# The residual's pieces of x in the FFN's gate and convolution tiles, squares of h over them, two buffers for the other squares

## The chip, the cores and the metric

The kernel runs on one core of one Trainium2 chip. The metric is the device time of one execution in microseconds (us). Of the kernel before there are three timed runs and one profiled execution.

## The reference

One inference step of one layer on 2048 frames of a prompt and 32 frames of a running stream, 1024 features wide. A mixer (stick-breaking attention with 8 heads of 64, and a state-space group) and a gated feed-forward network (FFN, width 2816, with a causal convolution of width 3 on the gate branch), each between two RMS norms. What this case touches is the sandwich of norms:

```python
def rmsnorm(x, g):
    x32 = x.astype(jnp.float32)
    y = x32 * lax.rsqrt(jnp.mean(x32 * x32, axis=-1, keepdims=True) + NORM_EPS)
    return (y * g.astype(jnp.float32)).astype(x.dtype)

# h = x + RMSNorm_post(Mixer(RMSNorm_pre(x)))
# y = h + RMSNorm_post2(ConvFFN(RMSNorm_pre2(h)))
```

The kernel must give y, the new keys and values, and the new states of the scan and of both convolutions, in float32.

## The kernel before

**Layout and precision.** Features lie on the 128 partitions, frames on the free axis. x, h and y are eight pieces of 128 features (c = 0 to 7). A dense matmul has float32 accuracy from three passes: both operands are split into a high and a low part (`xhi`, `xlo`, `w`), in `Kernel.dense` (L118 to L133; the matmuls are L124). Weights are split once, written back to HBM (`wS_out`, `wS_up`, `wS_dn`) and read from there later. The sums stand in PSUM tiles `o` and `u`, and in the last part of the program `t`.

**Stages.** The frames are cut into four super-blocks s = 0 to 3 of 512, 512, 512 and 544 columns. After the input projections, `Attention.heads` runs for each super-block in turn. Into the attention of super-block s+1 is woven, step by step, the rest of the work of super-block s: `Tail.stream`, a generator, which `Attention.fill` advances at a rate of its steps over the attention's slots. The stream of the last super-block runs alone at the end (`Tail.alone`).

**Attention in one line.** For each slot: scores z on PE (L811, two PSUM tiles), two sigmoids on ACT (`gam` L659, `beta` L660), a scan on DVE (`prow` L662), a product on POOL or DVE (L667), a transposition on PE (`pt` L832) and its copy (`wt` L835), then the sum over values (`pa` L847). A z tile is free again only when the scan that reads its first column is done.

**One stream.** A super-block has a half a and a half b of 256 columns (272 in the last). `Tail.stream` gives, in this order: eight steps of what the previous super-block still owes of its down projection; the output projection of half a (`out_units`, into tiles `m`, with squares of m summed in `msq`); the output projection of half b, with a step of the residual of half a after every fourth of its steps; the norm of h of half a (`root`); the residual of half b in one go; `split` of both halves into `xhi` and `xlo` (L958, L959); the norm of half b; the rest of what is owed; then `up` and `down` of the FFN by groups of columns, with steps of `finish` of the super-block before between them. What is left of the last down projection is owed to the next stream, and in the last super-block it is done at once, tile by tile, each with its `finish`.

**Residual** (L928 to L947). The norm's factor goes into `rm` (L201 in `rstd_steps` writes it). Then for each of the eight pieces: a tile `xr` (two buffers in the attention's scratch pool, eight in the pool `tl_late` for the last super-block; L938), the load of x from HBM (L939, in SP's queue), the scale of m by the gain and by `rm` (L940, DVE), the addition of x (L944, POOL for even c, DVE for odd c), the store of h to scratch in HBM (`hS`, L945, SP's queue), and the square of h.

**Square** (L764 to L772). The first square of a sum is written by ACT straight into it (L768). Every other is written by ACT into `sqt`, one buffer (L770, L771), and added by POOL (L772). Callers are the attention's output (`sq`), the output projection and the residual (`msq`), and `square_f` for the FFN's output (`fsq`).

**Up, down, finish.** `up` computes the gate column in `gb` (two buffers, 548 wide), its convolution in `y` (two buffers, 546 wide), the GeLU in steps on ACT, DVE and POOL (L1003 to L1013), and leaves `ah` and `al`. Between the last `up` of one super-block and the first of the next, `gb` and `y` hold nothing. `down` adds its sums to the tiles f, one buffer each: the first group is copied (L1057, ACT), the others are added (L1059, DVE). `finish` (L1067 to L1086) is the norm and residual of the FFN's output: factor `rstdf`, load of h into an `xr` tile (L1079), scale (L1080, DVE), addition (L1084), store of y. A new super-block's first copy into f waits for the stores of y of the one before.

**Order.** Each engine works through its instructions in one order, which a scheduler of the tile framework fixes when the program is built, from its own model of times and from the tiles that are free; a DMA is issued by SP in SP's order. Matmuls of the stream are held behind the last score or transposition written before them (`pin`).

Of the kernel before, what the change touches and what calls it, by code (L numbers as in the profile page):

```python
# [8 lines left out]
F32 = mybir.dt.float32  # L9
# [3 lines left out]
ALU = mybir.AluOpType  # L13
# [10 lines left out]
P = 128  # L24
# [584 lines left out]
class Attention:  # L609
# [151 lines left out]
                nc.gpsimd.tensor_tensor(lo[c][:, c0:c1], x, hi[c][:, c0:c1].bitcast(F32), op=ALU.subtract)  # L761
        return hi, lo

    def square(self, sq, x, first):  # L764

        nc = self.kn.nc
        if first:
            nc.scalar.activation(sq, x, AF.Square)  # L768
        else:
            t = self.tmp.tile([P, 272], F32, name="sqt")[:, : sq.shape[-1]]  # L770
            nc.scalar.activation(t, x, AF.Square)  # L771
            nc.gpsimd.tensor_tensor(sq, sq, t, op=ALU.add)  # L772

# [105 lines left out]
class Tail:  # L879
# [48 lines left out]
    def residual(self, s, half):  # L928

        kn, nc, att = self.kn, self.kn.nc, self.att  # L930
        t0 = SBS[s][0]
        c0, c1 = half
        n = c1 - c0
        rm = att.tmp.tile([P, 272], F32, name="rstd")
        kn.rstd_narrow(att.tmp, *kn.bank, [self.msq[:, c0:c1]], n, D, out=rm)
        yield
        for c, m in enumerate(self.m):
            x = (self.late or att.tmp).tile([P, 272], F32, name="xr", bufs=8 if self.late else 2)  # L938
            nc.sync.dma_start(x[:, :n], kn.a["xT"][:, c, t0 + c0 : t0 + c1])  # L939
            nc.vector.scalar_tensor_tensor(  # L940
                m[:, c0:c1], m[:, c0:c1], kn.col(C_GMIXP + c), rm[:, :n], op0=ALU.mult, op1=ALU.mult
            )
            eng = nc.vector if c % 2 else nc.gpsimd
            eng.tensor_tensor(m[:, c0:c1], m[:, c0:c1], x[:, :n], op=ALU.add)  # L944
            nc.sync.dma_start(kn.hS[s][:, c, c0:c1], m[:, c0:c1])  # L945
            att.square(self.msq[:, c0:c1], m[:, c0:c1], c == 0)
            yield  # L947

    def split(self, s, half):
# [118 lines left out]
    def finish(self, s, c0, c1, f):  # L1068

        kn, nc, att = self.kn, self.kn.nc, self.att  # L1070
        t0, n = SBS[s][0], c1 - c0
        r = att.tmp.tile([P, 272], F32, name="rstdf")
        for _ in kn.rstd_steps(
            att.tmp, *kn.bank, [self.fsq[:, c0:c1]], n, D, out=r, of=self.cols.pop((s, c0))
        ):
            yield
        for c in range(KC):
            h = (self.late or att.tmp).tile([P, 272], F32, name="xr", bufs=8 if self.late else 2)
            nc.sync.dma_start(h[:, :n], kn.hS[s][:, c, c0:c1])  # L1079
            nc.vector.scalar_tensor_tensor(  # L1080
                f[c][:, c0:c1], f[c][:, c0:c1], kn.col(C_GFFNP + c), r[:, :n], op0=ALU.mult, op1=ALU.mult
            )
            eng = nc.vector if c % 2 else nc.gpsimd
            eng.tensor_tensor(f[c][:, c0:c1], f[c][:, c0:c1], h[:, :n], op=ALU.add)  # L1084
            nc.sync.dma_start(kn.o["yT"][:, c, t0 + c0 : t0 + c1], f[c][:, c0:c1])
            yield  # L1086
# [208 lines left out]
```

## Time and profile before

| | us |
|---|---|
| median of three runs | 2998.81 |
| lowest and highest | 2997.21, 3003.68 |
| the profiled execution, its own time | 2999.56 |
| span in it, first to last instruction | 2997.4 |
| output projection of super-block 0, first residual's scales | from 812.27 |
| the last f squares of super-block 2, in the part that runs alone | 2560.9 to 2590.4 |

The mean granted clock of TensorE over the span is 0.979 of full speed. Engines: PE = TensorE matmul, PEld = its weight loads, DVE = VectorE, ACT = ScalarE, POOL = GpSimd, SP = SyncE, whose queue issues the DMAs (SPq). A row of the timeline reads: start, length, engine, line, operation, output <- inputs, shape, count, and in brackets the idle time just before it and what ended that. In a table of windows each engine has its busy time and its count of instructions, then come the granted clock, the share of DMA and GB/s.

### The profile page before, as it was taken

What the parts mean: (1) busy time and instruction counts of PE and PEld (TensorE: products, weight loads), DVE (VectorE), ACT (ScalarE), POOL (GpSimd) and SP (SyncE); (2) the same over time, 40 slices, a digit from 0 to 9 for tenths busy, and PEclk for the clock granted to TensorE, in tenths of its full rate; (3) what the DMA queues carried; (4) which work ended last, traced back from release to release, by engine and by line L of the source; (5) the groups of instructions that cost most, each with busy time, mean ns of one, the idle gap of its engine ahead of it and who ended that gap; (6) DMA issues with size and microseconds to landing.
All of it is one profiled execution on the core that took longest, in us unless ns stands there. A gap on an engine that the chain in (4) does not pass through costs nothing.

```text
span 2997.4 us, 43276 instructions
## 1 busy us (share of the span) xinstructions
PE 2839.3 (95%) x16175; PEld 2320.3 (77%) x16175; DVE 1567.7 (52%) x2386; ACT 1239.6 (41%) x2514; POOL 1254.8 (42%) x1077
## 2 busy tenths in 40 slices
PE   8999899989979999999999999999999999899996
PEld 6777778866757778886677777856777779799996
DVE  7676676546574544337734344485444543523334
ACT  5344444346675544337533333564333433312111
POOL 4555555245666665536522222454122224511113
PEclk9999999989989999999999999999999999899998
DMA  5645453657657777876455545645544455554555
GB/s 172 183 145 177 144 169 106 185 150 248 241 178 242 246 250 266 289 265 203 158 190 176 184 156 208 232 163 174 177 165 167 157 196 191 192 188 167 178 178 171
DMA packets 234659, 571.58 MB, mean 191 GB/s; under 512 B 49514, under 2 KB 101362, under 8 KB 205906
## 3 DMA queue, kind: packets, MB, share of 16 engines
q1 hardware_dynamic: 234450, 568.81, 57.2%
q8 instruction: 129, 2.11, 0.3%
q14 instruction: 80, 0.66, 0.1%
HBM read 435.22 MB, written 133.50 MB: 190 GB/s over the span
## 4 chain that ended last, share of the span: by engine, by line
PE 72%; DVE 14%; DMA 6%; issue 3%; ACT 3%; POOL 2%; SPq 1%; DVEq 0%; POOLq 0%; ACTq 0%
PE o L124 36%; PE u L124 11%; PE t L124 10%; PE pa L847 4%; PE z L811 3%; PE pt L832 3%; DVE prow L662 2%; PE o L365 2%; DVE xc L341 2%; DVE acB L436 1%; DMA xr<-hS 1%; DMA acB<-acD 1%; DVE xc L337 1%; DVE x L263 1%; DMA w<-wS_out 1%
## 5 line engine op out<-in xcount | busy, mean ns | idle before, releaser
L124 PE MATMUL o<-xhi,w 128*128 128x512 f32 (+2 forms) x3968 | 1039.6, 346 | 28.4 <-ACT xhi L287 7.9
L124 PEld LDWEIGHTS o<-xhi,w 128*128 128x128 f32 x3968 | 696.5, 191 | 129.6 <-issue 10.1
L124 PE MATMUL o<-xlo,w 128*128 128x512 f32 (+2 forms) x1984 | 684.9, 345 | 9.4 <-DVE xlo L959 4.1
L109 POOL TENSOR_TENSOR w<-wraw,w 128x1024 fp32r<-128x1024 f32 (+2 forms) x156 | 370.6, 2376 | 256.1 <-ACT w L108 233.3
L124 PEld LDWEIGHTS o<-xlo,w 128*128 128x128 f32 x1984 | 379.6, 191 | 56.8 <-DVE xlo L959 7.6
L667 POOL TENSOR_TENSOR beta<-beta,prow 128x512 f32<-128x512 f32 (+3 forms) x256 | 255.7, 1000 | 377.4 <-DVE prow L662 345.2
L124 PE MATMUL u<-xhi,w 128*128 128x512 f32 x1056 | 345.8, 398 | 0.8 <-ACT r L201 0.5
L124 PE MATMUL o<-ah,w 128*128 128x512 f32 x992 | 335.9, 401 | 3.3 <-ACT f L1057 2.6
L1013 POOL TENSOR_TENSOR y<-y,gb 128x512 f32<-128x512 f32 (+1 forms) x88 | 115.5, 1313 | 511.2 <-ACT gb L1012 509.2
L662 DVE TENSOR_TENSOR_SCAN prow<-gam,prow,z 128x513 f32<-128x513 f32 x192 | 244.8, 1277 | 108.7 <-ACT beta L660 103.2
L124 PEld LDWEIGHTS u<-xhi,w 128*128 128x128 f32 x1056 | 198.5, 188 | 56.1 <-issue 5.6
L659 ACT ACTIVATE gam<-z 128x512 f32<-128x512 f32 (+2 forms) x320 | 173.3, 542 | 128.1 <-PE z L811 83.0
L124 PEld LDWEIGHTS o<-ah,w 128*128 128x128 f32 x992 | 187.1, 189 | 49.8 <-ACT f L1057 3.6
L124 PE MATMUL u<-xlo,w 128*128 128x512 f32 x528 | 209.3, 396 | 0.0
L835 ACT COPY wt<-pt 128x512 f32<-128x512 f32 (+3 forms) x282 | 148.1, 532 | 144.0 <-PE pt L832 141.3
L1005 DVE SCALAR_TENSOR_TENSOR y<-gb,cv,y 128x512 f32<-128x512 f32 (+1 forms) x176 | 162.3, 923 | 78.4 <-ACT y L1003 75.6
L108 ACT CAST w<-wraw 128x1024 fp32r<-128x1024 f32 (+2 forms) x156 | 155.2, 995 | 114.5 <-PE o L124 63.7
L124 PE MATMUL o<-al,w 128*128 128x512 f32 x496 | 196.5, 396 | 0.0
L124 PE MATMUL t<-xhi,w 128*128 128x272 f32 x960 | 189.1, 292 | 2.3 <-DMA w<-wS_up 2.0
L832 PEld LDWEIGHTS pt<-ident,beta 128*128 128x128 f32 x1088 | 132.4, 144 | 67.8 <-issue 27.5
L832 PE MATMUL pt<-ident,beta 128*128 128x128 f32 x1088 | 177.4, 282 | 6.4 <-POOL beta L667 3.9
L124 PE MATMUL t<-ah,w 128*128 128x272 f32 (+1 forms) x768 | 160.1, 302 | 17.4 <-ACT f L1057 7.5
(262 smaller groups left out, 4845.9 us busy)
## 6 DMA issues: line engine op xcount, KB each, us to landing
w<-wS_up SPq DMA_DIRECT2D x132, 1024.0 KB, 4.8
w<-wS_dn SPq DMA_DIRECT2D x72, 768.0 KB, 4.8
wS_up<-w SPq DMA_DIRECT2D x44, 1024.0 KB, 4.8
w<-wS_out SPq DMA_DIRECT2D x39, 1024.0 KB, 6.3
wraw<-wup SPq DMA_DIRECT2D x44, 512.0 KB, 5.9
k<-kS SPq DMA_DIRECT2D x80, 256.0 KB, 4.0
wS_dn<-w SPq DMA_DIRECT2D x24, 768.0 KB, 4.5
w<-wS_dn SPq DMA_DIRECT2D x32, 512.0 KB, 4.4
```

The costliest lines, as they stand in the source:

```text
L108: nc.scalar.copy(hi[:, :n, :], raw[:, :n, :])
L109: nc.gpsimd.tensor_tensor(lo[:, :n, :], raw[:, :n, :], hi[:, :n, :].bitcast(F32), op=ALU.subtract)
L124: mm = nc.tensor.matmul(ps[:, : c1 - c0], l[:, k, :], at(r, k0 + k)[:, c0:c1], start=first and i == 0 and k == 0, stop=last and i == 2 and ...
L659: nc.scalar.activation(g[:, c0:512], z, AF.Sigmoid, scale=-0.125)
L662: nc.vector.tensor_tensor_scan(back(pr), back(g), z[:, 0:1].to_broadcast([P, n + 1]), self.kn.ones[:, 0:1] if prev is None else prev, op0= ...
L667: eng.tensor_tensor(b[:, :n], b[:, :n], pr[:, c0 + 1 : 513], op=ALU.mult)
L811: mm = nc.tensor.matmul(z[:, :n], q[:, P * b : P * b + P], k[:, :n], start=e == 0, stop=e == 1 and kc < s)
L832: mm = nc.tensor.transpose(t[:, P * j : P * j + P], w[:, P * j : P * j + P], kn.ident[:])
L835: copy(wt[:, : n // P, P * b : P * b + P], t[:, :n].rearrange("p (i q) -> p i q", q=P))
L847: nc.tensor.matmul(av[DH * (j % 2) : DH * (j % 2) + DH, c0:], v[:, j, :], wt[:, j, c0:], start=kc == s and j < 2, stop=kc == 0 and j > 1,)
L1005: nc.vector.scalar_tensor_tensor(y[:, :W], gb[:, i : i + W], kn.col(wc + i), y[:, :W], op0=ALU.mult, op1=ALU.add)
L1013: nc.gpsimd.tensor_tensor(y[:, :W], y[:, :W], t, op=ALU.mult)
```

## The change

`residual` takes, in the first three super-blocks, its pieces of x into the tiles `gb` and `y` of the FFN: pieces 0 and 1 into the two halves of a `y` tile, 2 and 3 into those of a `gb` tile, 4 and 5 into the second `y`, 6 and 7 into the second `gb`. In the last super-block the eight `xr` tiles stay. In all four the square of h is written over the piece of x, which has just been added, and not into `sqt`. `sqt` has two buffers for the other squares, and `finish` uses the name of the residual's factor (`rstd`) for its own. Behind L764 line numbers are higher by one, behind the residual by six.

```diff
--- before.py
+++ after.py
@@ -761,13 +761,14 @@
                 nc.gpsimd.tensor_tensor(lo[c][:, c0:c1], x, hi[c][:, c0:c1].bitcast(F32), op=ALU.subtract)
         return hi, lo
 
-    def square(self, sq, x, first):
+    def square(self, sq, x, first, t=None):
 
         nc = self.kn.nc
         if first:
             nc.scalar.activation(sq, x, AF.Square)
         else:
-            t = self.tmp.tile([P, 272], F32, name="sqt")[:, : sq.shape[-1]]
+            if t is None:
+                t = self.tmp.tile([P, 272], F32, name="sqt", bufs=2)[:, : sq.shape[-1]]
             nc.scalar.activation(t, x, AF.Square)
             nc.gpsimd.tensor_tensor(sq, sq, t, op=ALU.add)
 
@@ -935,15 +936,20 @@
         kn.rstd_narrow(att.tmp, *kn.bank, [self.msq[:, c0:c1]], n, D, out=rm)
         yield
         for c, m in enumerate(self.m):
-            x = (self.late or att.tmp).tile([P, 272], F32, name="xr", bufs=8 if self.late else 2)
-            nc.sync.dma_start(x[:, :n], kn.a["xT"][:, c, t0 + c0 : t0 + c1])
+            if self.late:
+                x = self.late.tile([P, 272], F32, name="xr", bufs=8)[:, :n]
+            else:
+                if c % 2 == 0:
+                    pair = self.yp.tile([P, 548], F32, name="gb") if c % 4 else self.yp.tile([P, 546], F32, name="y")
+                x = pair[:, 272 * (c % 2) : 272 * (c % 2) + n]
+            nc.sync.dma_start(x, kn.a["xT"][:, c, t0 + c0 : t0 + c1])
             nc.vector.scalar_tensor_tensor(
                 m[:, c0:c1], m[:, c0:c1], kn.col(C_GMIXP + c), rm[:, :n], op0=ALU.mult, op1=ALU.mult
             )
             eng = nc.vector if c % 2 else nc.gpsimd
-            eng.tensor_tensor(m[:, c0:c1], m[:, c0:c1], x[:, :n], op=ALU.add)
+            eng.tensor_tensor(m[:, c0:c1], m[:, c0:c1], x, op=ALU.add)
             nc.sync.dma_start(kn.hS[s][:, c, c0:c1], m[:, c0:c1])
-            att.square(self.msq[:, c0:c1], m[:, c0:c1], c == 0)
+            att.square(self.msq[:, c0:c1], m[:, c0:c1], c == 0, x)
             yield
 
     def split(self, s, half):
@@ -1069,7 +1075,7 @@
 
         kn, nc, att = self.kn, self.kn.nc, self.att
         t0, n = SBS[s][0], c1 - c0
-        r = att.tmp.tile([P, 272], F32, name="rstdf")
+        r = att.tmp.tile([P, 272], F32, name="rstd")
         for _ in kn.rstd_steps(
             att.tmp, *kn.bank, [self.fsq[:, c0:c1]], n, D, out=r, of=self.cols.pop((s, c0))
         ):
```

How the instructions stand is changed at three places. First SP's queue, around the loads of x for the first half of super-block 0 (`w<-wS_out` are loads of output weights, `hS<-m` the stores of h, `qa`, `k` and `v` belong to attention). Before:

```order
L104 DMA w<-wS_out_7385 128x2048
L945 DMA hS_101<-m_7284 128x256
L939 DMA xr<-xT 128x256
L945 DMA hS_101<-m_7285 128x256
L939 DMA xr<-xT 128x256
L104 DMA w<-wS_out_7436 128x2048
L945 DMA hS_101<-m_7286 128x256
L945 DMA hS_101<-m_7287 128x256
L939 DMA xr<-xT 128x256 x2
L104 DMA w<-wS_out_7486 128x2048
L828 DMA v<-vS_87 128x256
```

The same eight loads in the changed kernel:

```order
L945 DMA y<-xT 128x256 x2
L112 DMA wS_out_7385<-w 128x2048
L107 DMA wraw<-wout 128x1024
L945 DMA gb<-xT 128x256 x2
L945 DMA y<-xT 128x256 x2
L945 DMA gb<-xT 128x256
L807 DMA k<-kS_78 128x512
L945 DMA gb<-xT 128x256
```

Before, all but the first two loads stand one or two at a time behind stores of h; now all eight stand together, 38 to 45 rows of the queue ahead of the first store of h, and among the stores of split weights.

Second, DVE in the same half: the last of the eight scales, the four additions of x and what stands behind them (`prow` is the attention's scan, `xlo` the split). Before:

```order
L940 SCALAR_TENSOR_TENSOR m_7291<-m_7291,cv,rstd 128x256
L944 TENSOR_TENSOR m_7285<-m_7285,xr 128x256
L944 TENSOR_TENSOR m_7287<-m_7287,xr 128x256
L944 TENSOR_TENSOR m_7289<-m_7289,xr 128x256
L859 TENSOR_TENSOR att<-pa,att 64x512
L662 SCALAR_TENSOR_TENSOR prow<-gam_5853,ones,z 128x513
L662 SCALAR_TENSOR_TENSOR prow<-gam_5854,prow,z 128x513
L667 TENSOR_TENSOR beta<-beta,prow 128x512
L944 TENSOR_TENSOR m_7291<-m_7291,xr 128x256
```

In the changed kernel:

```order
L946 SCALAR_TENSOR_TENSOR m_7291<-m_7291,cv,rstd 128x256
L950 TENSOR_TENSOR m_7285<-m_7285,y 128x256
L950 TENSOR_TENSOR m_7287<-m_7287,gb 128x256
L950 TENSOR_TENSOR m_7289<-m_7289,y 128x256
L950 TENSOR_TENSOR m_7291<-m_7291,gb 128x256
L662 SCALAR_TENSOR_TENSOR prow<-gam_5853,prow,z 128x513
L662 SCALAR_TENSOR_TENSOR prow<-gam_5854,prow,z 128x513
L662 SCALAR_TENSOR_TENSOR prow<-gam_5855,ones,z 128x129
```

The fourth addition stood behind two scans and now stands ahead of them.

Third, POOL in the last super-block, around the residual of its half b, where the squares of super-block 2's FFN output (`fsq`) are added. Before:

```order
L944 TENSOR_TENSOR m_22314<-m_22314,xr 128x272
L944 TENSOR_TENSOR m_22316<-m_22316,xr 128x272
L944 TENSOR_TENSOR m_22318<-m_22318,xr 128x272
L944 TENSOR_TENSOR m_22320<-m_22320,xr 128x272
L772 TENSOR_TENSOR msq<-msq,sqt 128x272 x7
L772 TENSOR_TENSOR fsq<-fsq,sqt 128x256
L184 TENSOR_TENSOR rcol_23016<-rcol_23016,mhalf 128x3
L772 TENSOR_TENSOR fsq<-fsq,sqt 128x256 x6
L1013 TENSOR_TENSOR y<-y,gb 128x546 x2
```

In the changed kernel:

```order
L773 TENSOR_TENSOR fsq<-fsq,sqt 128x256 x7
L950 TENSOR_TENSOR m_22248<-m_22248,xr 128x272
L773 TENSOR_TENSOR fsq<-fsq,sqt 128x256
L950 TENSOR_TENSOR m_22250<-m_22250,xr 128x272
L950 TENSOR_TENSOR m_22252<-m_22252,xr 128x272
L950 TENSOR_TENSOR m_22254<-m_22254,xr 128x272
L773 TENSOR_TENSOR fsq<-fsq,sqt 128x256 x2
L773 TENSOR_TENSOR msq<-msq,xr 128x272 x3
L773 TENSOR_TENSOR fsq<-fsq,sqt 128x256
```

Seven of the 14 additions into `fsq` stand ahead of the residual's additions, and the others among its squares; before, all stood behind them.

## The prediction

> **What bounds the kernel now.** I read the page first: its busy shares, its slices, and its chain.
>
> ```profile
> PE 2839.3 (95%) x16175; PEld 2320.3 (77%) x16175; DVE 1567.7 (52%) x2386; ACT 1239.6 (41%) x2514; POOL 1254.8 (42%) x1077
> PE   8999899989979999999999999999999999899996
> PEclk9999999989989999999999999999999999899998
> PE 72%; DVE 14%; DMA 6%; issue 3%; ACT 3%; POOL 2%; SPq 1%; DVEq 0%; POOLq 0%; ACTq 0%
> ```
>
> PE is busy 2839.3 of 2997.4 us, so 158.1 us are idle, and a little more goes where the granted clock falls. The change alters no matmul. All it can win is idle PE time, and the slices (75 us each) show where that lies: the low ones are the twelfth (7, from 824 us), the 35th (8, from 2548 us) and the last (6, from 2923 us), and in the same three PEclk stands at 8. Then I read the waits, summed over the span (engine, line, what it waited for: us in total, times, longest).
>
> ```profile
> DVE m L944 <- DMA xr<-xT: 24.6, 10, 7.7
> PE z L811 <- DVE prow L662: 23.4, 28, 2.4
> ACT sqt L771 <- POOL msq L772: 24.0, 28, 2.2
> ACT sqt L771 <- POOL fsq L772: 21.1, 23, 4.8
> ```
>
> The first row is the wait that the change aims at, on DVE. The second is how DVE's lateness reaches PE: attention's score matmuls (z) wait for the scan (prow) to free one of two PSUM tiles. The last two are the single `sqt` tile: ACT can write the next square only after POOL has added the last one. ACT and POOL are busy 41% and 42% of the span, so these 45.1 us are mostly not on PE's path.
>
> **The change, part by part.** Every load, scale, add, store and square is still there, with the same shape, so nothing is removed and nothing is added: PE's 2839.3 us stay. What moves is when DVE, ACT, POOL and SP's queue do them.
>
> *A: super-block 0, first half.* The timeline of DVE and of SP's queue, and two windows (PE, PEld, DVE, ACT, POOL busy; granted clock; DMA share; GB/s):
>
> ```profile
> 812.27 3.74 DVE L940 SCALAR_TENSOR_TENSOR m<-m,cv,rstd 128x256 f32<-128x256 f32 x8 [4.13 <-ACT rstd L201]
> 819.68 0.43 DVE L944 TENSOR_TENSOR m<-m,xr 128x256 f32<-128x256 f32 x1 [3.34 <-DMA xr<-xT]
> 826.52 0.78 DVE L944 TENSOR_TENSOR m<-m,xr 128x256 f32<-128x256 f32 x1 [6.42 <-DMA xr<-xT]
> 816.73 0.43 SPq L939 DMA_DIRECT2D xr<-xT  x1
> 820.64 0.96 SPq L939 DMA_DIRECT2D xr<-xT  x2
> 828.21 1.45 SPq L939 DMA_DIRECT2D xr<-xT  x2
> 828.00:860.00 32.00, 23.46 (x120) 14.86 (x121) 23.30 (x27) 22.33 (x51) 21.93 (x22) 0.84 0.67 227
> 872.00:896.00 24.00, 18.67 (x85) 12.62 (x82) 20.72 (x31) 15.37 (x38) 14.52 (x19) 0.86 0.49 143
> ```
>
> The eight scales are done in 3.74 us, but with two `xr` tiles the loads are issued one or two at a time until 828.21, and DVE stands still 3.34 + 6.42 = 9.76 us before two of its four adds. The scans queue behind them on the same engine. In 828:860 PE is then idle 32.00 − 23.46 = 8.54 us and loses 23.46 × (1 − 0.84) = 3.75 us to the clock: 12.3 us. With the change the four tiles of the gate pool hold all eight pieces and are idle there, so the loads can be issued before the scales. DVE gets 9.76 us back, ahead of the stretch in which PE starves. Bounds: 0 and −12.3. DVE also has the second half of the out projection's scans to catch up with, whose work is unchanged, so I take half: **−6**.
>
> *B: super-block 0, second half.* In 872:896 PE loses 5.33 us idle and 18.67 × 0.14 = 2.6 us of clock, but DVE is busy 20.72 of 24 us there with scales, adds and the split, none of which goes. I bound this by 0 and half of it, −4, and take **−1**, near the first, since the busy DVE row is the nearer one.
>
> *C: super-blocks 1 and 2.* The two waits and the stretches behind or around them, with DVE's scales and the one stall of PE that the clock follows:
>
> ```profile
> 1346.72 0.68 DVE L944 TENSOR_TENSOR m<-m,xr 128x256 f32<-128x256 f32 x1 [3.15 <-DMA xr<-xT]
> 1924.40 0.43 DVE L944 TENSOR_TENSOR m<-m,xr 128x256 f32<-128x256 f32 x1 [7.68 <-DMA xr<-xT]
> 1389.35 4.33 DVE L940 SCALAR_TENSOR_TENSOR m<-m,cv,rstd 128x256 f32<-128x256 f32 x8
> 1394.92 0.79 PE L811 MATMUL z<-k,qa 128*128 128x512 f32 x1 [2.11 <-DVE prow L662]
> 1388.00:1404.00 16.00, 12.37 (x50) 7.01 (x48) 15.88 (x23) 10.90 (x25) 7.93 (x9) 0.79 0.44 149
> 1962.00:1998.00 36.00, 31.48 (x162) 19.41 (x162) 32.46 (x42) 26.72 (x62) 21.96 (x26) 1.00 0.62 202
> ```
>
> Here DVE waits 3.15 and 7.68 us for x in the first halves. PE pays in the second halves, where DVE is full: 3.63 us idle plus 12.37 × 0.21 = 2.6 us of clock in 1388:1404, that is 6.2, and 4.52 us in 1962:1998, together 10.7 us. In the new order the first half's chain ends sooner, and units of the last down projection that were used up before now stand beside the second half's residual. They are dense matmuls that PE can do while a scan is late. But DVE's load in those stretches (15.88 of 16 us) stays. Bounds 0 and −10.7; half: **−5**.
>
> *D: super-block 3.* The groups, waits and rows of the place where the new block's down projection first writes the f tiles:
>
> ```profile
> 2540.18 0.86 POOL L184 TENSOR_TENSOR rn_v<-rn_v,mhalf 128x3 f32<-128x3 f32 x1 [6.90 <-DVE rn_v L176]
> L772 POOL TENSOR_TENSOR fsq<-fsq,sqt x14: 723/738/1152, 2560.9 to 2589.7; 128x256 f32<-128x256 f32 x14
> 2608.40 5.22 DVE L1080 SCALAR_TENSOR_TENSOR f<-f,cv,rstdf 128x256 f32<-128x256 f32 x8 [0.31 <-ACT rstdf L201]
> ACT f L1057 <- DMA o_yT<-f: 6.9, 2, 5.6
> PE t L124 <- ACT f L1057: 7.5, 1, 7.5
> 2604.00:2620.00 16.00, 8.04 (x48) 7.65 (x47) 9.98 (x25) 3.91 (x11) 6.99 (x7) 0.68 0.74 231
> ```
>
> The 14 squares of super-block 2's f are added between 2560.9 and 2590.4 us, behind the residual's squares, all through one `sqt`. Its final norm therefore ends late (scales at 2608.40), the stores of y later, and the first copy into an f tile waits for them; PE waits 7.5 us for that copy. The window's loss is 7.96 us idle + 8.04 × 0.32 = 2.6 us of clock = 10.5 us. With two `sqt` tiles most of these squares move ahead of the second residual, into time in which POOL waits (6.90 us in one piece), and the final norm can end some 17 us earlier, twice the stall and more. Bounds 0 and −10.5. What replaces the stall is the supply of activations to the same down projection, so I leave a third: **−7**.
>
> *E: the tail.* In the last tile one scale group takes 5.42 us of DVE, and squares go in steps of ACT, then POOL:
>
> ```profile
> 2980.61 0.43 ACT L771 ACTIVATE sqt<-f 128x272 f32<-128x272 f32 x1 [0.87 <-POOL fsq L772]
> 2981.12 0.76 POOL L772 TENSOR_TENSOR fsq<-fsq,sqt 128x272 f32<-128x272 f32 x1 [0.54 <-ACT sqt L771]
> 2974.00:2982.00 8.00, 1.09 (x7) 0.87 (x7) 5.93 (x12) 1.72 (x4) 5.17 (x7) 0.76 0.65 198
> ```
>
> A step of 0.43 + 0.87 = 1.30 us shrinks to POOL's own 0.76 at best, 0.54 each. Seven to eight such steps would give −4, if all are behind the last matmul; PE's gap in 2974:2982 has its cause in DVE (5.93 of 8 us). I take **−1**, bounds 0 and −4.
>
> Edits at nothing: the shared `rstd` name lets the final norm wait for readers of the residual's factor, which are over long before. The gate's tiles are needed again by the first up unit, after the residual's last square; that unit's result needs the norm of those squares anyway, so the wait hides behind it. The cost if the cover goes is one square, 0.76 us.
>
> Sum: −6 − 1 − 5 − 7 − 1 = **−20**. The profiled execution took 2999.56 us (span 2997.4, 2.16 around it), 0.75 above the median of 2998.81 that runs without it show, so 2979.6, rounded to 2980.
>
> **A rule weighed on the clock.** Two 4 us windows show what an interrupted PE costs afterwards:
>
> ```profile
> 880.00:884.00 4.00, 4.00 (x13) 3.32 (x14) 3.38 (x6) 1.50 (x4) 2.56 (x4) 0.50 0.26 79
> 1396.00:1400.00 4.00, 3.21 (x11) 2.37 (x10) 4.00 (x5) 2.39 (x7) 2.36 (x3) 0.50 0.45 131
> ```
>
> Both run at a granted clock of 0.50 although PE is busy. The Trainium skill ("TensorE: Matmul & The Clock Gate", section "HAM oscillation — how this bites in real kernels") says that PE gaps over about 3.4 us bring the half clock. The wait row before the second window is 2.11 us and the idle time of its 16 us is 3.63, so the trace has the half clock behind a shorter single wait too. By the page only gaps over its limit would count: the sum would keep A and D and lose C's 2.6 us of clock, some 1 us less gain in the middle value.
>
> **Rivals.**
>
> *R1, covered anyway (0.14).* DVE's waits for x vanish but PE is limited by DVE's work in these stretches. For it: DVE at 15.88 of 16 us in 1388:1404, which no load changes. Against it: 9.76 us of pure DVE standstill just ahead of 828:860. Only D and E come, −8: 2992.
>
> *R2, nothing comes of it (0.09).* The loads stand behind other entries in SP's queue that wait (weights, the gate's tiles), and land no sooner. For it: PE waits for weights in this place already, 3.78 us in the row below. Against: the four tiles are idle when the residual starts. D's stall would also stay, if the first norm is not what is late. 2999.
>
> ```profile
> 1296.80 0.58 PE L124 MATMUL o<-xhi,w 128*128 128x256 f32 x1 [3.78 <-DMA w<-wS_out]
> L944 DVE TENSOR_TENSOR m<-m,xr x32: 389/430/1503, 815.9 to 2552.6; 128x256 f32<-128x256 f32 x24, 128x272 f32<-128x272 f32 x8
> L944 POOL TENSOR_TENSOR m<-m,xr x32: 723/908/968, 812.8 to 2549.4; 128x256 f32<-128x256 f32 x24, 128x272 f32<-128x272 f32 x8
> ```
>
> *R3, slower by bunching (0.10).* With x always there, eight scales (4.33 us) and four adds (4 × 0.43) stand on DVE in one block of 6 us with no scan between, where a wait used to let the scheduler put scans. PE has two z tiles, some 2 us of cover. Each such block would then make a gap like that of 1388:1404, 6.2 us with its clock. Four new ones, in both halves of super-blocks 1 and 2, cost 25; A and C do not come, D and E give −8: +17, 3016. It decides when the block outlasts z's two tiles by about 3 us. Against it: eight scales in one block exist already (rows 812.27 and 1389.35), and only the second is followed by a gap at once.
>
> *R4, DVE and POOL adds collide (0.05).* Packed adds run on both engines at the same time. DVE's add has a median of 0.430 us and a longest of 1.503, so something holds it at times. If 16 of the 24 adds of the first three super-blocks each lose a POOL add, 0.908, DVE loses 14.5 us in full stretches; A and C are eaten, D, E and B give −9: +5.5, 3005. The Trainium skill ("SBUF — State Buffer", section "Who interferes with whom") says that a DVE instruction with two SBUF inputs and a GpSimd one that reads SBUF hold an exclusive lock against each other, which speaks against packing the adds; the median near the shortest, 0.389, says that most adds do not meet it today.
>
> **How the numbers follow.** The forecast of 2980 has 0.62, with a range of its own of 2966 to 2990; R1 0.14, R2 0.09, R3 0.10, R4 0.05. All lower ends together give 2999.6 − 41.5 = 2958; A to E will not all be full, and I set the low end to 2964, leaving out under 0.05. The high end of 3001 takes in R1 and R2 and leaves R3 and R4. A measurement of this kernel can tell about 0.2%, 6 us: 2992.8 to 3004.8 is "same". Faster: the forecast and 0.08 of R1, 0.70. Same: the rest of R1 (0.06), R2 (0.09) and 0.02 of R4, 0.17. Slower: R3 and 0.03 of R4, 0.13.
>
> **What would show it.** Right: DVE's wait for x is under 3 us in total; PE's idle time in the 32 us behind the first chain falls under 5 us with a clock over 0.9; the first copy into f no longer waits for stores of y; the time of ACT's waits for POOL's square adds falls by half. Wrong: DVE's adds no longer wait, but PE's wait for prow stays at 23 us or grows (R1, R3); DVE's adds after the scales take near 1 us (R4); the new loads take long from issue to landing or hold up weights behind them (R2). The forecast as a whole falls if D's stall stays, or if a new gap of over 3 us stands in super-blocks 1 or 2.

## The result, and the profile after

The changed kernel takes 2974.8 us in the median of six runs (2971.92 to 2983.65), beside 3005.93 for the kernel before in the same two sets of runs (2997.21 to 3010.91). The ratio is 0.9912, with a 95% interval of 0.9894 to 0.9929, so 21 to 32 us are gained. The profiled execution took 2975.94 us, 23.6 less than that of the kernel before.

The page of the changed kernel (busy shares, slices of 74 us):

```profile
PE 2832.0 (95%) x16175; PEld 2327.7 (78%) x16175; DVE 1576.6 (53%) x2386; ACT 1238.4 (42%) x2514; POOL 1256.1 (42%) x1077
PE   8999999989989999999999999999999999999996
PEclk9999999989999999999999999999999999999998
```

The 35th slice, which stood at 8 in PE and in PEclk, stands at 9 in both now. The twelfth stands at 8 in PE, 7 before, with its clock at 9, 8 before. The waits of the changed kernel, summed over the span:

```profile
PE z L812 <- DVE prow L662: 16.5, 14, 3.4
ACT sqt L772 <- POOL fsq L773: 9.9, 17, 1.4
```

DVE's wait for x, 24.6 us before, is in no row any more. ACT's waits for POOL's adds before it can write the next square, 45.1 us before, are 9.9, and PE's for the scan fall from 23.4 to 16.5 us, in half as many pieces, but with a longest of 3.4 us where it was 2.4.

To see in which part of the program the time was won, I set two landmarks that stand in every version: PE's first score of super-block 1, where the stream of super-block 0 begins, and PE's first matmul into a tile t, where the last super-block starts to run alone. First the kernel before (start, length, engine, line, operation):

```profile
726.60 0.22 PE L811 MATMUL z<-k,qa 128*128 128x128 f32 x1
2460.97 0.50 PE L124 MATMUL t<-ah,w 128*128 128x512 f32 x1
2985.09 1.43 PE L195 MATMUL u<-ident,rn_v 128*128 128x128 f32 x6 [2.00 <-DVE rn_v L186]
```

The same three rows of the changed kernel:

```profile
725.10 0.22 PE L812 MATMUL z<-k,qa 128*128 128x128 f32 x1
2447.80 0.50 PE L124 MATMUL t<-ah,w 128*128 128x512 f32 x1
2961.42 1.43 PE L195 MATMUL u<-ident,rn_v 128*128 128x128 f32 x6 [2.00 <-DVE rn_v L186]
```

The **woven part**, from the first landmark to the second (super-blocks 0 to 2), was 1734.4 us and is 1722.7. The **last part**, from the second to the end of PE's last instruction, was 525.6 and is 515.0. So about half of the gain lies in each. Each stretch holds the same matmuls in every version, and all versions below are measured with these two stretches. Much of what two runs of one program differ lies ahead of the first landmark: it comes at 725.10 us here and at 734.49 in a second run (e12), whose span is 9.0 us longer.

### The profile page after: what moved, and what is told of

The parts are those of the page before. It is cut to its first block, busy times and chain, and to the rows that moved or that the text cites. A ratio compares the mean times of both kernels' runs of the same rounds, so it can differ in the third digit from the quotient of the medians.

```text
span 2973.7 us, 43439 instructions
## 1 busy us (share of the span) xinstructions
PE 2832.0 (95%) x16175; PEld 2327.7 (78%) x16175; DVE 1576.6 (53%) x2386; ACT 1238.4 (42%) x2514; POOL 1256.1 (42%) x1077
## 4 chain that ended last, share of the span: by engine, by line
PE 76%; DVE 12%; DMA 5%; ACT 2%; issue 2%; POOL 1%; SPq 1%; DVEq 0%; POOLq 0%; ACTq 0%
PE o L124 37%; PE u L124 12%; PE t L124 11%; PE pa L848 4%; PE z L812 4%; PE pt L833 3%; PE o L365 2%; DVE xc L341 2%; DVE prow L662 1%; DMA w<-wS_out 1%; DVE acB L436 1%; DVE x L263 1%; DVE f L1086 1%; DMA acB<-acD 1%; DVE xc L337 1%
## 5 line engine op out<-in xcount | busy, mean ns | idle before, releaser
L662 DVE TENSOR_TENSOR_SCAN prow<-gam,ones,z 128x129 f32<-128x129 f32 (+3 forms) x128 | 112.1, 877 | 126.1 <-ACT beta L660 119.8
```

What stands on the lines that cost most here:

```text
L662: nc.vector.tensor_tensor_scan(back(pr), back(g), z[:, 0:1].to_broadcast([P, n + 1]), self.kn.ones[:, 0:1] if prev is None else prev, op0= ...
```

## The experiments

The theory at the start: the placement carries the woven part, the second `sqt` the last part. In the table, "over x" means squares written over the piece of x. Ratios are against the kernel before on the same chip.

| label | what differs from the kernel before | ratio (95%) | woven part | last part |
|---|---|---|---|---|
| (before) | nothing | 1 | 1734.4 | 525.6 |
| e4 | shared factor name | 0.9998 (0.9986 to 1.0011) | 1733.5 | 525.0 |
| e1 | placement | 0.9966 (0.9952 to 0.9979) | 1726.5 | 524.1 |
| e3 | two sqt | 0.9905 (0.9875 to 0.9935) | 1725.2 | 514.6 |
| e8 | three sqt, factor name | 0.9905 (0.9885 to 0.9924) | 1720.6 | 511.1 |
| e2 | two sqt, over x in the last super-block, factor name | 0.9913 (0.9887 to 0.9938) | 1720.4 | 515.7 |
| e6 | own tile for f's squares | 0.9979 (0.9965 to 0.9993) | 1735.8 | 521.8 |
| e7 | own tile for m's squares | 0.9968 (0.9957 to 0.9979) | 1730.6 | 519.4 |
| e9 | over x in the last super-block | 0.9956 (0.9941 to 0.9971) | 1734.5 | 514.1 |
| e10 | over x in all | 0.9921 (0.9909 to 0.9934) | 1724.0 | 514.3 |
| e5 | placement, over x in all, factor name | 0.9891 (0.9870 to 0.9912) | 1715.3 | 514.4 |
| (after) | e5 and two sqt | 0.9912 (0.9894 to 0.9929) | 1722.7 | 515.0 |
| e12 | the changed kernel again | 0.9914 (0.9901 to 0.9927) | 1724.3 | 513.0 |
| e11 | e5 and an own tile for f's squares | 0.9881 (0.9868 to 0.9893) | 1711.2 | 512.7 |

The stretches repeat within 2 us where a program is run twice (before and e4, whose instructions stand in the same order on all engines; after and e12).

### The parts alone: e1 to e4

e1, the placement alone:

```diff
-            x = (self.late or att.tmp).tile([P, 272], F32, name="xr", bufs=8 if self.late else 2)
-            nc.sync.dma_start(x[:, :n], kn.a["xT"][:, c, t0 + c0 : t0 + c1])
+            if self.late:
+                x = self.late.tile([P, 272], F32, name="xr", bufs=8)[:, :n]
+            else:
+                if c % 2 == 0:
+                    pair = self.yp.tile([P, 548], F32, name="gb") if c % 4 else self.yp.tile([P, 546], F32, name="y")
+                x = pair[:, 272 * (c % 2) : 272 * (c % 2) + n]
+            nc.sync.dma_start(x, kn.a["xT"][:, c, t0 + c0 : t0 + c1])
```

> The placement alone: x of super-blocks 0 to 2 goes into the gate tiles; squares stay in a single sqt, finish keeps rstdf. My theory (early loads free DVE in super-blocks 0 to 2, the two sqt tiles free the FFN's f tiles in 3): gain 12 to 17 us against the kernel before, DVE waits for x under 3 us in super-blocks 0 to 2, and the first copy into f in super-block 3 still waits for stores of y, about 7.5 us on PE. Rival (the squares' ping-pong through one sqt is what held the residual): gain under 5 us. Rival (any edit reshuffles the whole order and the time moves by chance): no stage keeps the gain it has in the changed kernel.

Measured: 10 us (6 to 14), 7.9 in the woven part and 1.5 in the last. PE's waits behind 2500 us, of this kernel:

```profile
PE t L124 <- ACT f L1062: 7.0, 1, 7.0
```

So the wait for the copy into f stays, as expected, and DVE has no wait for x left in super-blocks 0 to 2; the gain is a little below its band.

e2, the changed kernel without the placement:

```diff
-                if c % 2 == 0:
-                    pair = self.yp.tile([P, 548], F32, name="gb") if c % 4 else self.yp.tile([P, 546], F32, name="y")
-                x = pair[:, 272 * (c % 2) : 272 * (c % 2) + n]
+                x = att.tmp.tile([P, 272], F32, name="xr", bufs=2)[:, :n]
...
-            att.square(self.msq[:, c0:c1], m[:, c0:c1], c == 0, x)
+            att.square(self.msq[:, c0:c1], m[:, c0:c1], c == 0, x if self.late else None)
```

> The changed kernel without the placement: x of super-blocks 0 to 2 goes into two xr tiles as before, their squares through the two sqt; squares over x in super-block 3 and the shared factor name stay. My theory: gain 7 to 10 us, all of it behind 2500 us, where PE's wait of 7.5 us for the copy into f goes; DVE waits for x stay near 24 us. Rival (two sqt tiles matter in all super-blocks): gain 15 or more, with part of it in super-blocks 0 and 1.

Measured: 26 us, as much as the whole change, and 14.0 of them in the woven part. My theory falls here: without the placement the woven part gains too, and DVE's wait for x is 17.1 us, not near 24.

e3, in `square`:

```diff
-            t = self.tmp.tile([P, 272], F32, name="sqt")[:, : sq.shape[-1]]
+            t = self.tmp.tile([P, 272], F32, name="sqt", bufs=2)[:, : sq.shape[-1]]
```

> Only sqt with two buffers. My theory: this is what lets the squares of f move ahead in super-block 3, so PE's wait for the copy into f falls to under 2 us and the gain is 6 to 9 us. Rival (the squares over x in super-block 3 free the single sqt and are the cause there): gain under 3 us, the wait stays.

Measured: 28 us (20 to 38), where 6 to 9 were expected. Its two stretches give 20 of them; its profiled run was the slowest of its four. The last part gains 11.0, the woven part 9.2. PE's wait for the copy into f falls to 3.6 us, not under 2 as expected. DVE and PE in this kernel:

```profile
DVE m L944 <- DMA xr<-xT: 20.8, 11, 5.6
PE z L811 <- DVE prow L662: 27.0, 31, 3.4
```

DVE waits for x nearly as long as before (24.6), and the woven part is shorter all the same. So that wait was not the only thing that could be won there.

e4, in `finish`:

```diff
-        r = att.tmp.tile([P, 272], F32, name="rstdf")
+        r = att.tmp.tile([P, 272], F32, name="rstd")
```

> Only the name of finish's factor changes to the residual's, so that the two share a tile. My theory: within 3 us of the kernel before, since the readers of the other factor are long over. Rival (chance of the order): moves by 5 us or more in either direction, in stages that the name doesn't touch.

Measured: no difference (4 us either way at most). The name is worth nothing.

### Whose squares: e5 to e8

After these four, three theories. Theory 1: the second `sqt` is what gains, above all for f's squares. Theory 2: the residual's burst of squares must not go through a tile that it shares. Theory 3: each sum needs two tiles, so that ACT writes one while POOL adds the other.

The edits of e5 (in the changed kernel), e6 and e7 (in the kernel before, `square` taking the tile's name as an argument) and e8 (in the kernel before):

```diff
e5
-                t = self.tmp.tile([P, 272], F32, name="sqt", bufs=2)[:, : sq.shape[-1]]
+                t = self.tmp.tile([P, 272], F32, name="sqt")[:, : sq.shape[-1]]
e6
-            self.att.square(self.fsq[:, a:b], self.f[c][:, a:b], c == 0)
+            self.att.square(self.fsq[:, a:b], self.f[c][:, a:b], c == 0, "sqf")
e7
-            att.square(self.msq[:, c0:c1], m[:, c0:c1], i == 0)
+            att.square(self.msq[:, c0:c1], m[:, c0:c1], i == 0, "sqm")
-            att.square(self.msq[:, c0:c1], m[:, c0:c1], c == 0)
+            att.square(self.msq[:, c0:c1], m[:, c0:c1], c == 0, "sqm")
e8
-            t = self.tmp.tile([P, 272], F32, name="sqt")[:, : sq.shape[-1]]
+            t = self.tmp.tile([P, 272], F32, name="sqt", bufs=3)[:, : sq.shape[-1]]
-        r = att.tmp.tile([P, 272], F32, name="rstdf")
+        r = att.tmp.tile([P, 272], F32, name="rstd")
```

> The changed kernel with sqt back to one buffer; placement and squares over x stay, in all super-blocks. Theory 1, after the first four runs (the second sqt is what gains, above all because the squares of f in super-block 3 no longer go through one tile): near the placement alone, 0.996 to 0.998 of the kernel before, and PE's wait of about 7 us for the copy into f is back. Theory 2 (it is the residual's squares that must not share sqt with the rest, and squares over x are as good as a second tile): 0.990 to 0.993, wait for the copy into f under 4 us.

Measured: 0.9891, just under the band of theory 2, with 1.0 us of PE's wait for the copy into f left. Theory 1 falls, theory 2 holds: with the residual's squares over x, a second `sqt` isn't needed. How the squares run shows in POOL's rows of the last super-block's first residual, first in the kernel before:

```profile
2514.51 0.77 POOL L772 TENSOR_TENSOR msq<-msq,sqt 128x272 f32<-128x272 f32 x1 [0.54 <-ACT sqt L771]
2515.82 0.77 POOL L772 TENSOR_TENSOR msq<-msq,sqt 128x272 f32<-128x272 f32 x1 [0.55 <-ACT sqt L771]
```

and then in e5, where the three are one row:

```profile
2495.36 2.84 POOL L773 TENSOR_TENSOR msq<-msq,xr 128x272 f32<-128x272 f32 x3
```

Through the one tile a square costs ACT and POOL in turn, 1.31 us; over x POOL goes from one to the next, 0.95 us each, and ACT's waits for additions into `msq` are 2.5 us in the whole span, 24.0 before. The residual's eight squares are a burst, and it stands in the order of two engines that attention uses too.

> The kernel before with a square tile of its own for the squares of f alone; the residual's, the output projection's and the attention's squares share the one sqt. Theory 1: super-block 3 gains about as much as with two sqt, 8 to 12 us between the start of its residual and its up projection, and the other stages stay within 4 us: 0.995 to 0.998. Theory 2: under 3 us in that place.

Measured: 6 us, in the band of the ratio, but the last part gains 3.8 where 8 to 12 were expected. PE's waits behind 2500 us:

```profile
PE o L124 <- DVE y L1022: 3.7, 1, 3.7
PE t L124 <- DVE xlo L959: 2.6, 2, 2.4
PE t L124 <- ACT f L1057: 0.4, 1, 0.4
```

The wait for the copy into f is nearly gone, but one of 3.7 us (1.2 before) for the product of a gate column and the old one for `xlo` stand there: the residual of the last super-block still takes as long, 38 us from the scales of its first half to those of its second in both kernels.

> The kernel before with a square tile of its own for the squares of m (output projection and residual); the squares of f and the attention's share the other. Theory 1: super-block 3 gains as in the run with a tile for f's squares, since f's and m's squares are apart in both: 8 to 12 us, and super-block 2 some 5 us more, as with two sqt: 0.992 to 0.996. Theory 3 (two tiles for one sum matter, so that ACT writes a square while POOL adds the last): under 4 us in all, since each sum has one tile.

Measured: 10 us, 3.8 in the woven part and 6.2 in the last, outside the bands of both theories. Keeping the sums apart gives something, but a burst through one tile remains a burst through one tile.

> The kernel before with three sqt and the shared factor name, no placement. If two buffers already let ACT run ahead of POOL, a third gives no more: within 4 us of the run with two sqt alone, 0.989 to 0.992. If the squares of three users at once (attention, m, f) are what collides, another 3 to 6 us: 0.987 to 0.989.

Measured: 0.9905, the ratio of the run with two. By the ratios two are enough. The stretches don't settle it: they are 4.6 and 3.5 us shorter than in e3, whose profiled run was its slowest.

### Squares and placement one by one: e9 to e12

e9 and e10, in the kernel before, with `square` taking a tile as in the change:

```diff
e9
-            att.square(self.msq[:, c0:c1], m[:, c0:c1], c == 0)
+            att.square(self.msq[:, c0:c1], m[:, c0:c1], c == 0, x[:, :n] if self.late else None)
e10
-            att.square(self.msq[:, c0:c1], m[:, c0:c1], c == 0)
+            att.square(self.msq[:, c0:c1], m[:, c0:c1], c == 0, x[:, :n])
```

> The kernel before with one edit: in super-block 3 alone the residual's squares are written over its pieces of x; all others go through the one sqt, x of super-blocks 0 to 2 stays in the two xr tiles. Theory 2 (the residual's squares must not share a tile with those of f and of the output projection): PE's wait for the copy into f falls under 2 us, super-block 3 gains 9 to 13 us, the earlier ones stay within 4 us: 0.995 to 0.997. Rival (the gain of super-block 3 needs a free tile from earlier on): under 4 us.

Measured: 13 us, 11.5 of them in the last part and nothing in the woven part: just what theory 2 expects. PE's wait for the copy into f in this kernel:

```profile
PE t L124 <- ACT f L1058: 0.6, 1, 0.6
```

> The kernel before with the residual's squares over x in all super-blocks, but x still in two xr tiles: no placement, one sqt. If the squares carry the gain and early loads of x give nothing on top: 0.989 to 0.992, as with placement and squares over x. If each gives its own part: 0.992 to 0.995, the placement alone being worth 0.0034. If two xr tiles, held until POOL has added the square, delay the loads of x: DVE's waits for x rise over 30 us, and 0.996 or more.

Measured: 24 us. The last part is that of e9; the woven part gains 10.4, and these come from squares over x in super-blocks 0 to 2, with x still in two tiles. DVE's wait for x falls rather than rises:

```profile
DVE m L945 <- DMA xr<-xT: 15.4, 11, 3.5
```

The interval spans two of the three cases. The woven part decides it: with the placement on top (e5) it is another 8.7 us shorter, so each gives its own part.

e11, in the changed kernel, with `square` taking the tile's name:

```diff
-                t = self.tmp.tile([P, 272], F32, name="sqt", bufs=2)[:, : sq.shape[-1]]
+                t = self.tmp.tile([P, 272], F32, name=tag)[:, : sq.shape[-1]]
...
-            self.att.square(self.fsq[:, a:b], self.f[c][:, a:b], c == 0)
+            self.att.square(self.fsq[:, a:b], self.f[c][:, a:b], c == 0, tag="sqf")
```

> Placement and squares over x, one sqt for attention and output projection, and a tile of their own for the squares of f. PE's and DVE's order is that of the run with one sqt. If the two sqt cost super-block 0 about 5 us, as the stages of four profiles say, and a tile for f's squares keeps super-block 3's gain: as the run with one sqt or up to 3 us better, 0.987 to 0.990, and faster than the changed kernel by 2 to 8 us. Rival: the differences between these are noise, within 0.2% of the changed kernel.

> The changed kernel once more, beside the three above on the same chip: 0.990 to 0.992 of the kernel before, as measured first.

Measured: e11 0.9881 (2969.1 us), e12 0.9914 (2977.5 us), on the same chip, with intervals that don't meet. e11 is 8.4 us faster than the changed kernel, just above its band, and uses no more memory than the change. All of its lead but some 2 us lies in the woven part, and all of e5's. So on top of placement and squares over x the second `sqt` costs something there. It lies at the start. The first 204 us behind the first landmark (PE, PEld, DVE, ACT, POOL busy; clock; DMA share; GB/s) in the changed kernel:

```profile
725.10:929.10 204.00, 179.18 (x1042) 139.41 (x1041) 125.39 (x166) 125.26 (x279) 137.26 (x131) 0.92 0.65 221
```

The same stretch of e12, its second run:

```profile
734.49:938.49 204.00, 177.85 (x1034) 137.91 (x1033) 123.61 (x165) 125.21 (x279) 135.94 (x131) 0.92 0.65 218
```

That of e5, with one `sqt`:

```profile
728.93:932.93 204.00, 182.82 (x1072) 141.20 (x1070) 125.74 (x172) 126.88 (x288) 141.07 (x134) 0.94 0.67 227
```

That of e11:

```profile
733.28:937.28 204.00, 180.27 (x1089) 139.81 (x1088) 126.72 (x173) 129.52 (x295) 142.75 (x135) 0.97 0.68 231
```

And those of the kernel before and of e10, for later:

```profile
726.60:930.60 204.00, 178.82 (x1066) 134.70 (x1065) 129.31 (x176) 132.96 (x303) 138.01 (x138) 0.94 0.63 213
729.28:933.28 204.00, 184.20 (x1105) 138.30 (x1104) 130.84 (x180) 136.09 (x310) 144.54 (x141) 0.96 0.66 223
```

With two `sqt` PE gets 1042 and 1034 matmuls done in that time, in e5 1072 and in e11 1089. I count what PE loses as its idle time plus its busy time times what is missing of the clock: 24.8 + 14.3 = 39.2 us in the changed kernel and 26.2 + 14.2 = 40.4 in e12, against 32.1 in e5 and 29.1 in e11. These 7 to 11 us are nearly all that the woven parts differ by (7 to 13), and against e11 most of them are clock.

One wait of PE goes with the second tile in every version. It is 3.8 us long in the five with two or three `sqt`, and 0.5 to 1.1 us in the nine with one. DVE and PE around it, and the clock behind it, in the changed kernel:

```profile
760.02 3.93 DVE L598 SCALAR_TENSOR_TENSOR xc<-xc,cv,rstd 128x544 f32<-128x544 f32 x4
763.87 0.68 DVE L667 TENSOR_TENSOR beta<-beta,prow 128x512 f32<-128x512 f32 x1
764.47 0.15 DVE L176 TENSOR_SCALAR rn_v<-u 128x2 f32<-128x2 f32 x1
764.70 1.09 PE L833 MATMUL pt<-ident,beta 128*128 128x128 f32 x4 [3.80 <-DVE rn_v L176]
765.10:775.10 10.00, 8.86 (x35) 6.89 (x34) 8.62 (x11) 6.90 (x18) 10.00 (x12) 0.50 0.37 144
```

Four of attention's transpositions wait while DVE works through four scales of the state-space group's norm, and the granted clock behind them is 0.50: in the 10 us that begin 40 us after the first landmark it is 0.50 to 0.56 in all five versions, and 0.69 to 1.00 in the other nine. In e11 these 10 us are:

```profile
773.28:783.28 10.00, 10.00 (x75) 9.47 (x75) 7.64 (x11) 8.42 (x20) 9.86 (x11) 0.88 0.11 31
```

So the second tile's cost is in large part this wait and the clock behind it. Why the scheduler's order has this wait when there is a second tile stays open.

## Why the prediction was right, and where its reasons were not

**The sum.** Forecast 2980 for the profiled execution's own time, measured 2975.94; forecast 2966 to 2990 as the likeliest case's own range. By stretches: A, B and C were −6 − 1 − 5 = −12, and the woven part gave −11.7 (−10.1 in the second run); D and E were −8, and the last part gave −10.6 (−12.6). Both sizes hold, but the first by luck: it came at other places, and from other causes, than the ones given.

**A to C, early loads.** The loads do come early, and DVE's wait goes. DVE in the changed kernel, super-block 0, first half, and the first and last load in SP's queue:

```profile
823.68 5.18 DVE L946 SCALAR_TENSOR_TENSOR m<-m,cv,rstd 128x256 f32<-128x256 f32 x8 [4.12 <-ACT rstd L201]
828.78 0.96 DVE L950 TENSOR_TENSOR m<-m,y 128x256 f32<-128x256 f32 x1
829.67 0.96 DVE L950 TENSOR_TENSOR m<-m,gb 128x256 f32<-128x256 f32 x1
830.55 0.96 DVE L950 TENSOR_TENSOR m<-m,y 128x256 f32<-128x256 f32 x1
831.43 0.41 DVE L950 TENSOR_TENSOR m<-m,gb 128x256 f32<-128x256 f32 x1
739.37 0.86 SPq L945 DMA_DIRECT2D y<-xT  x2
745.99 0.43 SPq L945 DMA_DIRECT2D gb<-xT  x1
```

The window of 32 us behind the start of that chain, in the same kernel:

```profile
824.00:856.00 32.00, 27.97 (x185) 22.04 (x183) 21.76 (x29) 21.50 (x52) 26.41 (x27) 0.89 0.90 312
```

The loads are issued 78 to 84 us ahead of the scales, and the four additions follow them without a gap. In those 32 us PE loses 4.03 us idle and 27.97 × 0.11 = 3.1 of clock, 7.1 against 12.3 before. I asked for under 5 us idle with a clock over 0.9: the first holds, the second just fails. But the stretch around it gains nothing. A and B, −7 together, lie in the first 204 us of the woven part, and there the kernel before loses 25.2 + 10.7 = 35.9 us by the rows above (38.3 in e4) and the changed kernel 39.2 and 40.4. An estimate from the traces, each matmul counted at its median spacing in the kernel before, has the changed kernel 1 us late (e12: 3) some 200 us behind the first landmark, and 11 us ahead (e12: 10) at the second. So the gain came in super-blocks 1 and 2, where C was −5. In B's place PE even waits longer, behind a block of eight scales:

```profile
859.82 5.49 DVE L946 SCALAR_TENSOR_TENSOR m<-m,cv,rstd 128x256 f32<-128x256 f32 x8
867.43 0.47 PE L812 MATMUL z<-k,qa 128*128 128x128 f32 x1 [3.44 <-DVE prow L662]
```

Taken by itself (e1), the placement shortens the woven part by 7.9 us, two thirds of the 12 that A to C forecast for it.

**The step that failed** is in the reading of the waits: "these 45.1 us are mostly not on PE's path". ACT and POOL were busy 41% and 42%, and I took that share for slack. But the squares come in bursts, at the place where DVE and PE are pressed too, and on engines that work in order. Squares over x alone (e10) shorten the woven part by 10.4 us, most of it in the first 204 us (27.2 us lost there, 35.9 before). What counted were the residual's squares: in e10 ACT's wait behind `msq` falls from 24.0 to 1.5 us, and that behind `fsq` rises from 21.1 to 26.2. Nor is such a sum the price: in e1 the wait behind `msq` rises to 42.0 us, and the woven part is 7.9 shorter all the same. The second `sqt` in the changed kernel, which I also put at nothing there, costs 7 to 9 (1715.3 in e5, 1722.7 and 1724.3 with it). Placement and squares over x make 19 together (e5), the second tile takes 7 to 9 of them back, and 10 to 12 are left, near the 12 forecast. The two missing terms nearly cancelled. What part of the 10 is ACT's shorter waits, and what part the order that the scheduler makes of them, stays open, since each edit changes both.

**D, the stall at f.** Right in its mechanism, with the size −7 a little too small and too narrow a cause. The scales of the last two norms of super-block 2's f on DVE's timeline, in the changed kernel:

```profile
2561.05 5.81 DVE L1086 SCALAR_TENSOR_TENSOR f<-f,cv,rstd 128x256 f32<-128x256 f32 x8 [0.40 <-ACT rstd L201]
2574.52 4.71 DVE L1086 SCALAR_TENSOR_TENSOR f<-f,cv,rstd 128x256 f32<-128x256 f32 x8 [0.31 <-ACT rstd L201]
```

PE's largest waits between 2500 and 2640 us, in the same kernel:

```profile
PE t L124 <- DVE f L1065: 2.8, 1, 2.8
PE o L124 <- DVE y L1028: 2.7, 1, 2.7
```

The second norm starts 34 us earlier (2608.40 before), of which 13 are gained ahead of the last part; the wait of 7.5 us for the copy into f is gone, and 2.8 and 2.7 us, for a sum into f and a gate column, are late next. I gave the cause as the two `sqt` tiles. They do it alone (e3, with 3.6 us of the wait left), but so do squares over x alone (e9, with one `sqt`), to within 1 us in the last part: the change does the same thing twice.

**E, the tail.** PE's last matmul of the up projection parts E from D. In the kernel before and in the changed one it is

```profile
2939.51 0.29 PE L124 MATMUL o<-xhi,w 128*128 128x272 f32 x1
2916.81 0.29 PE L124 MATMUL o<-xhi,w 128*128 128x272 f32 x1
```

From the second landmark to it are 478.5 us before and 469.0 after (469.1 in e12), and from it to the end 47.0 and 46.0 (43.9). So D gave −9.5, inside its bounds, and E −1.0 (−3.1), with −1 forecast. E's mechanism shows in the last matmuls that wait for a sum of squares, before and after:

```profile
2981.93 1.16 PE L166 MATMUL u<-ones,fsq 128*128 128x1 f32 x6 [4.24 <-POOL fsq L772]
2958.69 0.74 PE L166 MATMUL u<-ones,fsq 128*128 128x1 f32 x6 [1.95 <-POOL fsq L773]
```

**The edits at nothing.** The factor's name: 0.9998, right. The gate's tiles, at most one square of 0.76 us: too small. With the squares in them, ACT waits for POOL at the gate's first copies after the residual of super-block 0:

```profile
878.88 0.19 ACT L987 COPY gb<-fhist 128x2 f32<-128x2 f32 x1 [4.14 <-POOL msq L773]
```

In e5 and e11 such waits are 0.6 us in all. Whether PE paid for the 4.14 is not shown.

**The rivals.** R1 (covered anyway) has its half-truth: DVE's waits for x can stay, at 20.8 us in e3, and the woven part still shortens by 9. R2 (nothing comes of it) is excluded by the loads' place in the queue. R3 (bunching) came once, not four times: the 3.44 us behind the eight scales in super-block 0 (row 867.43); in super-blocks 1 and 2 PE's waits for the scan fall from 10.8 to 4.8 us, the longest 2.8. R4 (DVE and POOL collide) did come, but not at its price: below.

## What to carry to other kernels

A scratch tile with one buffer between two engines makes them take turns, and when such work comes in a burst on engines that work in order, the price isn't read from their busy share: look at what the bracket behind each row of the burst names, and at who stands behind it. Two edits that remove the same wait don't add up, and the second may cost something: here placement, squares over x and second tile were worth 10, 24 and 28 us alone, all three 26, and the first two with a tile for f's squares in place of the second `sqt` 36. Where a scheduler orders the program, measure parts alone and together, with landmarks that stand in every version.

## What the runs showed of the hardware that was not expected

DVE is slower beside POOL. By line and form (busy us, mean ns; idle time before and its releaser), the scales and additions of the first three super-blocks in the kernel before:

```profile
L940 DVE SCALAR_TENSOR_TENSOR m<-m,cv,rstd 128x256 f32<-128x256 f32 x48 | 23.8, 564 | 12.4 <-ACT rstd L201 12.4
L944 DVE TENSOR_TENSOR m<-m,xr 128x256 f32<-128x256 f32 x24 | 16.0, 665 | 24.6 <-DMA xr<-xT 24.6
```

The scales in the changed kernel, in the same view:

```profile
L946 DVE SCALAR_TENSOR_TENSOR m<-m,cv,rstd 128x256 f32<-128x256 f32 x48 | 32.5, 746 | 9.3 <-ACT rstd L201 9.3
```

And what POOL does there while the four additions of the timeline above run:

```profile
828.54 0.92 POOL L950 TENSOR_TENSOR m<-m,gb 128x256 f32<-128x256 f32 x1 [0.36 <-DVE m L946]
829.42 0.92 POOL L773 TENSOR_TENSOR msq<-msq,sqt 128x256 f32<-128x256 f32 x1
830.30 0.92 POOL L773 TENSOR_TENSOR msq<-msq,y 128x256 f32<-128x256 f32 x1
```

Three additions beside POOL's take 0.96 us each, and the fourth, which starts at 831.43 when POOL is done, 0.41. The scales used to run while POOL stood mostly still (one addition of 0.91 us beside the eight scales from 812.27); now its additions and squares run beside them, and they cost 8.7 us more in all. The Trainium skill ("SBUF — State Buffer", section "Who interferes with whom") says that a DVE instruction with two SBUF inputs and a GpSimd one that reads SBUF contend for one port; this trace agrees, 0.96 against 0.41. R4 priced this at 14.5 us of DVE time and put all of it on the path. It was 8.7 on the scales with nothing added on the additions (15.1 us busy, 16.0 before), and DVE saved 24.6 us of waiting.
